# Hybrid encoder layer on one core: four column tiles in the opening, later lane arithmetic, an earlier split of the down activations

## The chip, the core and the metric

One NeuronCore of a Trainium2 chip runs the whole layer as one program. TensorE multiplies; VectorE (DVE in the profile) and ScalarE (ACT) do the elementwise work; GpSimd (POOL) and SyncE (SP) mostly issue DMAs. The metric is the device time of one execution in microseconds; the kernel before takes 2270.38 us (median of 3 runs, 2269.89 to 2271.57).

## The reference, cut to what matters

Two requests of 256 tokens are computed together as T = 512 tokens of width 2048, in float32. The layer is

```
xn    = rmsnorm(x);  proj = xn @ w_in                  # 7200 columns: NA q,k,v; GDN q,k,v; z; b,a
y_na  = neighbourhood_attention(q, k, v)               # 8 heads of 128
y_dn  = gated_deltanet_bidir(conv+silu(q,k,v), z, b, a)  # 8 heads, chunks of 64, both directions
h     = x + [y_na ; y_dn] @ w_out
hn    = rmsnorm(h)
y     = rmsnorm(h + (silu(hn @ w_gate) * (hn @ w_up)) @ w_down)   # 5632 hidden columns
```

In the delta rule each head needs, for each chunk, products of k with k and of k with q, a triangular solve of 64 x 64, and decays made from b and a (the "gates").

## The kernel before, in words

**Products.** Every float32 operand is split in two float32r parts: `hi` is a rounded copy that ScalarE makes, `lo` is the rest that VectorE makes by a subtraction (`split`, L126 to L133). A product is three matmuls, hi by hi, hi by the other's lo, lo by the other's hi (`mm3`, L150), each 128 x 128 weights by 128 x 512 tokens. A column tile (128 output columns) takes 16 k-tiles, thus 48 matmuls (`col_tile`, `half_gemm`); its weights come in two halves of 512 KB over SP's queue into three `raw` buffers and are split into three `hi` and three `lo` buffers.

**The opening** (L223 to L328). 12 small matmuls on ones run while the first data comes. SP's queue loads `nwm`, then a first piece of the weights of column tile 0, x for the first two k-tiles (`xr[0]`, one transfer of 512 KB), the same piece of column tile 1, the weights `ba_raw` of b and a, and then the other seven x transfers with the rest of the two column tiles' weights between them. Column tiles 0 and 1 (k and q of GDN head 0) are multiplied two k-tiles (one pair) at a time for four pairs, then the last eight k-tiles tile by tile. Small matmuls for b and a (`ba_gemm`) follow every fourth k-tile. At the end `token_rstd` squares x (ScalarE), adds the squares up (VectorE), sums over partitions by one matmul on ones and makes `rstd`. x stays in SBUF as hi and lo.

**After the opening.** For GDN heads 0 to 7 the k and q columns are multiplied, convolved and put through silu (`conv_silu`: VectorE scales a tile out of PSUM, and four multiply-adds and two ScalarE operations follow); head 0 takes the two tiles of the opening, the others call `col_tile`. Then come the 24 column tiles of neighbourhood attention, then v and z of the GDN heads with the recurrence. Small work is laid between the matmuls by hand: generators in `chains` and `side` go one step forward with each `pump()`, which `half_gemm` calls after every second k-tile, so eight times a column tile. `kq_post(h)` waits a number of steps (`KQ_START` = 20 for head 0, `KQ_GAP` = 8 for the others), then computes the products of k with k and q through three PSUM tiles of pool `psm` (three banks, tag `s`). Column tiles lie in pool `pg` (three banks).

`gates()` (L385) is traced after head 0's columns: some 45 small VectorE and ScalarE operations with DMAs between them. `lanes()` is the triangular solve: 128 lanes, one per direction, head and chunk, on VectorE. It is started when the last `kq_post` is done, and goes one step forward twice in a column tile (`advance(vector_work)`). Its first step issues ten DMAs that gather `kkq` and `qq`; the arithmetic follows in the next steps (L485 on). Its result goes out to DRAM (L576) and comes back in `prepare` for the recurrence.

**The MLP down product.** The 5632 hidden columns are cut in four segments of 512, done directly (`down`, 8 pairs of output tiles with 24 matmuls per tile pair), and two groups of 14, done by a seven-product Strassen form (`down_group`, j = 0 to 7). The order is `down(0)`, group 0, `down(1)`, group 1, `down(2)`, and the last segment. `down` reads a split activation tile `sA`. While group g runs, `load_act` (L1131) loads the next segment's activations into `sA` by DMA, and at the last j splits them: two ScalarE copies (L1137) and two VectorE subtractions (L1138). In `down_group` this call, `after()`, stands behind the fifth product (`pb`, S2) and the additions that follow it (L1280 to L1283).

**What sets the order.** TensorE's order is that of the program text. On the other engines a planner orders the instructions by its own times: an instruction runs as soon as the planner takes it as ready and its engine as free, and of several the one that was traced first. `tc.high_priority(offset=AHEAD)` lets an instruction count as traced 120 instructions earlier (weight splits use it). `pin` (`keep_in_program_order`) puts an instruction behind the one traced just before it on its engine; the four instructions of `load_act` are pinned. Once planned, each engine's order is fixed.

Of the kernel before, what the change touches and what calls it, by code (L numbers as in the profile page):

```python
# [8 lines left out]
F32 = mybir.dt.float32  # L9
F32R = mybir.dt.float32r  # L10
# [32 lines left out]
NA_START = 5  # L43
NA_GAP = 8
PV_GAP = 4
KQ_START = 20
KQ_GAP = 8
CORE_START = 2
N_GAP = 1
# [13 lines left out]
def hybrid_encoder(ctx: ExitStack, tc: tile.TileContext, xT, w_in, w_ba, w_out, w_gate,  # L63
# [156 lines left out]
    def sm_tile():  # L220
        return psm.tile([P, T], F32, tag="s", name="ps_s")

    kkq = cp.tile([P, C, 2, C], F32, tag="c", name="kkq")  # L223
    rstd = wk.tile([P, T], F32, tag="rstd", name="rstd")


# [2 lines left out]
    xr = [ini.tile([P, 2, T], F32, tag=f"xr{j}", name="x_raw") for j in range(8)]  # L229
    ba_raw = wp.tile([P, KT, 32], F32, tag="raw", bufs=3, name="ba_raw")  # L230
    baw = ini.tile([P, KT, 32], F32, tag="baw", name="ba_w")
    w0 = [[ini.tile([P, 8, P], F32, tag=f"w{c}{i}", name="w0_raw") for i in range(2)]
          for c in range(2)]

    def split_x(j):
        for i in range(2):
            k = 2 * j + i
            split(xs[k][0], xs[k][1], xr[j][:, i], nwm[:, k:k + 1])

    def fetch_w0(i, k0, k1):  # L240
        for c in range(2):
            nc.sync.dma_start(w0[c][i][:, k0:k1], w_in[c, i][:, k0:k1])

    nc.sync.dma_start(w0[0][0][:, :2], w_in[0, 0][:, :2])
    nc.sync.dma_start(xr[0], xT[0])
    nc.sync.dma_start(w0[1][0][:, :2], w_in[1, 0][:, :2])
    nc.sync.dma_start(ba_raw, w_ba)
    for j in range(1, 8):
        nc.sync.dma_start(xr[j], xT[j])
        if j == 1:  # L250
            fetch_w0(0, 2, 8)
        if j == 3:
            fetch_w0(1, 0, 8)

    def token_rstd():
        acc = ini.tile([P, T], F32, tag="acc", name="ssq_acc")
        for k in range(KT):
            sq = acc if k == 0 else ini.tile([P, T], F32, tag="sq", bufs=2, name="x_sq")
            act(out=sq, in_=xr[k // 2][:, k % 2], func=AF.Square)
            if k:  # L260
                tt(acc, acc, sq, ALU.add)
        ps = sm_tile()
        mm(ps, ones, acc, start=True, stop=True)
        rstd_bcast(ps, rstd, ini)
        ini_cm.__exit__(None, None, None)

    def evac(ps, tag, bufs=1, pool=None):
        t = (pool or wk).tile([P, T], F32, tag=tag, bufs=bufs, name="ev_" + tag)
# [6 lines left out]
    def ba_gemm(ks):  # L275
        for k in ks:
            g = k % 4 * 32
            mm(ps_ba[g:g + 32], baw[:, k], xr[k // 2][:, k % 2], start=(k < 4), stop=(k >= KT - 4),
               skip_group_check=True)

    ps_w = sm_tile()
    for _ in range(IDLE):
        mm(ps_w[:, :P], ones, ones, start=True, stop=True)
    ps0 = [pg.tile([P, T], F32, tag="g", name="ps_g") for _ in range(2)]

    def w0_pair(parts):
        hi = wp.tile([P, 8, P], F32R, tag="hi", bufs=3, name="w_hi")
        lo = wp.tile([P, 8, P], F32R, tag="lo", bufs=3, name="w_lo")
        for c, i, k0, k1 in parts:
            split(hi[:, k0:k1], lo[:, k0:k1], w0[c][i][:, k0:k1])  # L290
        return hi, lo

    def first_tiles(c, w, ks):
        for k in ks:
            mm3(ps0[c], w[0][:, k % 8], w[1][:, k % 8], xs[k][0], xs[k][1], k == 0, k == KT - 1)

    hl = [[wp.tile([P, 8, P], F32R, tag=t, bufs=3, name="w_" + t) for t in ("hi", "lo")]
          for _ in range(2)]

    def split_w0(c, k0, k1):  # L300
        split(hl[c][0][:, k0:k1], hl[c][1][:, k0:k1], w0[c][0][:, k0:k1])

    split_w0(0, 0, 2)
    split_x(0)
    split_w0(1, 0, 2)
    for j in range(4):
        ks = (2 * j, 2 * j + 1)
        if j:
            split_x(j)
        if j == 1:  # L310
            for c in range(2):
                split_w0(c, 2, 8)
            tt(baw, ba_raw, nwm[:, :, None].broadcast_to([P, KT, 32]), ALU.mult)
        for c in range(2):
            first_tiles(c, hl[c], ks)
        if j % 2:
            ba_gemm(range(2 * j - 2, 2 * j + 2))
    for j in range(4, 8):
        split_x(j)
    for c in range(2):  # L320
        w = w0_pair([(c, 1, 0, 8)])
        first_tiles(c, w, range(8, KT))
        ba_gemm(range(8 + 4 * c, 12 + 4 * c))
    ps_k0, ps_q0 = ps0
    token_rstd()
    ba = wk.tile([P, T], F32, tag="xi", bufs=2, name="ba")
    tt(ba, ps_ba, rstd, ALU.mult)
    nc.gpsimd.dma_start(s_ba.rearrange("g r t -> (g r) t"), ba)  # L328
# [139 lines left out]
    def lanes():  # L468
# [5 lines left out]
                                .rearrange("d h b k f s c -> (d h b k f) (s c)"))  # L474
        for d in range(2):
            nc.gpsimd.dma_start(qq[half[d]], s_qq.rearrange("h (j t) -> (h j) t", t=C))
        yield


        def vtt(*a):  # L480
# [98 lines left out]

    for h in range(H):  # L580
        kq = wk.tile([P, 2, T], F32, tag="kq", bufs=2, name="kq")
        ps = ps_k0 if h == 0 else col_tile(w_in[2 * h], xs)
        conv_silu(ps, 8 + h, kq[:, 0])
        ps = ps_q0 if h == 0 else col_tile(w_in[2 * h + 1], xs)
# [12 lines left out]
        chains.append(kq_post(h, kq, sqh, sql))  # L597
# [388 lines left out]
    def ahead(lead=AHEAD):  # L986
        return tc.high_priority(offset=lead)
# [252 lines left out]
    def down_group(g, X, sums, after):  # L1240
        A11, A12, A22, S4, S3, S1, S2 = range(7)
        plain = fetch_plain(g, 0)
        for j in range(8):
            first, second = sums
            b11, b21, b22 = plain
            if j < 7:
                sums = fetch_sums(g, j + 1)
                plain = fetch_plain(g, j + 1)
            if g == 1 and j:
                add_residual(j - 1)  # L1250
            h = hT[j].rearrange("p f (b t) -> p (f b) t", b=2)
# [12 lines left out]
            nc.scalar.copy(p7, pc)  # L1264
            with ahead():
                w = w_split(first)
            product(pd, w, X, S1, True)
            tt(d, pd, p7, ALU.subtract)
            with ahead():
                w = w_split(b21)  # L1270
            product(pa, w, X, A12, False, True)
            for q in range(2):
                tt(h[:, 0], h[:, 0], pa[:, q], ALU.add)
            with ahead():
                tt(first, first, b22, ALU.add)
                w = w_split(first)
            product(pb, w, X, S2, True, True)
            u2 = dq.tile([P, L], F32, tag="u2", name="u2d")
            plus_both(u2, p1, pb)
            tt(h[:, 1], h[:, 1], u2, ALU.add)  # L1280
            tt(h[:, 2:], h[:, 2:], u2[:, None, :].broadcast_to([P, 2, L]), ALU.subtract)
            for q in range(2):
                tt(h[:, 3], h[:, 3], d[:, q], ALU.add)  # L1283
            if j == 7:
                after()
            with ahead():
                w = w_split(b22)
# [174 lines left out]
```

## Time and profile before

| | |
|---|---|
| median of 3 runs | 2270.38 us |
| profiled execution: its time, its span | 2270.45 us, 2268.6 us |
| mean granted TensorE clock | 0.997 |
| VectorE, ScalarE, GpSimd busy | 77%, 47%, 16% of the span |
| DMA | 400.77 MB, 177 GB/s over the span |

The span goes from the first to the last instruction. Busy shares are means over stages with different limits. Matmuls overlap in the pipeline, so that one row's duration (about 0.39 us for 512 columns) is longer than the distance from one start to the next. Times are microseconds from the span's start, mean durations in groups are in ns. In a timeline row the first number is the start, the second the duration (of all xN merged), and brackets at the end give the idle time of the engine before it and what ended it. The granted clock is 1.00 at 2.4 GHz and 0.50 at 1.2 GHz.

### The profile page before, as it was taken

Reading aid. Unit: us, or ns where it says so; the run is one execution under the profiler, and the core shown is the slowest. Engines: PE = TensorE matmul, PEld = TensorE weight load, DVE = VectorE, ACT = ScalarE, POOL = GpSimd, SP = SyncE. Lnnn points to the kernel's source line nnn. Section 1 sums busy time; section 2 is a strip of 40 time slices with the busy share of each in tenths; the row PEclk is TensorE's granted clock in tenths of the full one; section 3 lists DMA queues with packets and bytes.
Section 4 is the critical chain, followed back from the end, with each engine's and each line's share of the span. In section 5 each row is a group of like instructions: output and inputs, shape, how many; then the busy total and the mean of one; then the engine's idle time right before and its main releaser. Section 6 shows DMA issues by size and latency. Waiting matters only on the chain.

```text
span 2268.6 us, 32159 instructions
## 1 busy us (share of the span) xinstructions
PE 2247.9 (99%) x12004; PEld 1932.9 (85%) x12004; DVE 1752.7 (77%) x2665; ACT 1056.5 (47%) x1554; POOL 368.1 (16%) x584
## 2 busy tenths in 40 slices
PE   9999999999999999999999999999999999999997
PEld 7888888888888888888888888888888888888877
DVE  7654699994555537888888888888888788898866
ACT  6777232324434416644444444444444454444435
POOL 1423300014433001111111111111010011102100
PEclk9999999999999999999999999999999999999999
DMA  5544522246544547777777777767777577669742
GB/s 207 154 149 138 196 99 91 100 140 180 148 136 135 209 149 237 204 195 214 202 203 200 197 211 186 214 188 213 203 198 185 170 216 184 180 203 219 191 149 75
DMA packets 130124, 400.77 MB, mean 177 GB/s; under 512 B 17664, under 2 KB 30368, under 8 KB 129968
## 3 DMA queue, kind: packets, MB, share of 16 engines
q1 hardware_dynamic: 88576, 271.89, 35.2%
q0 software_dynamic: 41392, 126.83, 25.5%
q8 instruction: 95, 1.56, 0.3%
q14 instruction: 61, 0.50, 0.1%
HBM read 358.47 MB, written 40.17 MB: 176 GB/s over the span
## 4 chain that ended last, share of the span: by engine, by line
PE 97%; DMA 1%; DVE 1%; ACT 0%; issue 0%; SPq 0%; POOL 0%; DVEq 0%; POOLq 0%; ACTq 0%
PE ps_g L75 38%; PE ps_d L75 14%; PE ps_a L75 14%; PE ps_c L75 14%; PE ps_b L75 7%; PE ps_s L75 7%; PE ps_s L78 1%; PE ps_o L75 1%; DMA s_uq<-kkq 0%; DMA nml<-s_na 0%; DMA lead<-s_uq 0%; DVE hT L1357 0%; DMA x_raw<-in_xT_dram 0%; DVE w_lo L130 0%; ACT w_hi L129 0%
## 5 line engine op out<-in xcount | busy, mean ns | idle before, releaser
L75 PE MATMUL ps_g<-xhi,w_hi 128*128 128x512 f32 x896 | 365.1, 408 | 1.0 <-ACT xhi L132 0.5
L75 PE MATMUL ps_g<-xhi,w_lo 128*128 128x512 f32 x896 | 350.0, 391 | 0.4 <-DVE w_lo L130 0.4
L75 PE MATMUL ps_g<-xlo,w_hi 128*128 128x512 f32 x896 | 349.3, 390 | 0.4 <-DVE xlo L133 0.3
L130 DVE TENSOR_TENSOR w_lo<-w_raw,w_hi 128x1024 fp32r<-128x1024 f32 (+2 forms) x170 | 205.5, 1209 | 109.2 <-ACT w_hi L129 97.9
L129 ACT ACTIVATE w_hi<-b 128x1024 fp32r<-128x1024 f32 (+1 forms) x180 | 185.6, 1031 | 221.2 <-issue 99.6
L129 ACT ACTIVATE w_hi<-w_raw 128x1024 fp32r<-128x1024 f32 (+2 forms) x170 | 178.0, 1047 | 219.9 <-PE ps_g L75 174.2
L129 ACT ACTIVATE w_hi<-w_first 128x1024 fp32r<-128x1024 f32 x132 | 140.0, 1061 | 212.0 <-PE ps_c L75 139.5
L130 DVE TENSOR_TENSOR w_lo<-b,w_hi 128x1024 fp32r<-128x1024 f32 (+1 forms) x180 | 212.9, 1183 | 1.5 <-ACT w_hi L129 1.2
L75 PEld LDWEIGHTS ps_g<-xhi,w_lo 128*128 128x128 f32 x896 | 168.2, 188 | 37.7 <-DVE w_lo L130 1.4
L75 PEld LDWEIGHTS ps_g<-xhi,w_hi 128*128 128x128 f32 x896 | 168.5, 188 | 36.6 <-ACT xhi L132 2.5
L75 PEld LDWEIGHTS ps_g<-xlo,w_hi 128*128 128x128 f32 x896 | 168.6, 188 | 32.8 <-DVE xlo L133 1.0
L130 DVE TENSOR_TENSOR w_lo<-w_first,w_hi 128x1024 fp32r<-128x1024 f32 x132 | 161.3, 1222 | 37.2 <-ACT w_hi L129 34.4
L75 PE MATMUL ps_c<-xc,w_hi 128*128 128x512 f32 x704 | 176.7, 393 | 0.0
L75 PE MATMUL ps_d<-xc,w_hi 128*128 128x512 f32 x704 | 176.3, 392 | 0.0
L75 PE MATMUL ps_a<-xc,w_hi 128*128 128x512 f32 x704 | 176.3, 392 | 0.0
L75 PEld LDWEIGHTS ps_c<-xc,w_hi 128*128 128x128 f32 x704 | 126.7, 189 | 23.1 <-issue 0.2
L75 PEld LDWEIGHTS ps_a<-xc,w_hi 128*128 128x128 f32 x704 | 126.7, 189 | 22.7
L75 PEld LDWEIGHTS ps_d<-xc,w_hi 128*128 128x128 f32 x704 | 126.6, 189 | 22.6
L75 PEld LDWEIGHTS ps_c<-xc,w_lo 128*128 128x128 f32 x704 | 96.0, 190 | 6.9
L75 PEld LDWEIGHTS ps_d<-xc,w_lo 128*128 128x128 f32 x704 | 96.0, 190 | 6.9
L75 PEld LDWEIGHTS ps_a<-xc,w_lo 128*128 128x128 f32 x704 | 96.0, 190 | 6.9
L129 ACT ACTIVATE w_hi<-w_two 128x896 fp32r<-128x896 f32 x64 | 61.0, 952 | 86.2 <-PE ps_c L75 31.0
(410 smaller groups left out, 4464.9 us busy)
## 6 DMA issues: line engine op xcount, KB each, us to landing
w_raw<-in_w_in_dram SPq DMA_DIRECT2D x110, 512.0 KB, 3.4
b<-in_w_gate_dram SPq DMA_DIRECT2D x66, 512.0 KB, 3.9
b<-in_w_up_dram SPq DMA_DIRECT2D x66, 512.0 KB, 5.1
b<-in_w_group_dram SPq DMA_DIRECT2D x48, 448.0 KB, 4.9
w_raw<-in_w_out_dram SPq DMA_DIRECT2D x32, 512.0 KB, 3.6
w_raw<-in_w_down_dram SPq DMA_DIRECT2D x32, 512.0 KB, 3.9
w_two<-in_w_group_dram SPq DMA_DIRECT2D x32, 448.0 KB, 5.8
w_two<-in_w_group_dram POOLq DMA_DIRECT2D x32, 448.0 KB, 6.4
```

Of the source, the lines that this page charges most:

```text
L75: pin(nc.tensor.matmul(*a, **k))
L78: pin(nc.tensor.transpose(*a))
L129: act(out=hi, in_=src, func=AF.Copy)
L130: tt(lo, src, r32(hi), ALU.subtract)
```

## The change: what it does

1. The opening multiplies four column tiles (k and q of GDN heads 0 and 1) instead of two, one pair of k-tiles at a time for all eight pairs. Their raw weights lie in one tile `w0` of the pool `cp` (its slot belongs to `kkq` later). On SP's queue each pair's weights (4 x 128 KB, 1 KB per row) go ahead of the pair's x (512 KB); for the first pair the order is weights of tile 0, half of x, weights of tiles 1 to 3, the other half of x. Two of the four accumulators lie in `pg`, two in `psm`.
2. The squares of x are traced two pairs behind the splits, and `token_rstd` before the last pair's matmuls.
3. `KQ_START` goes from 20 to 12; heads 0 and 1 both take tiles of the opening.
4. In `lanes()` three steps instead of one lie between the issue of the gathers and the arithmetic.
5. In `down_group`, `after()` moves from behind the fifth product's additions to behind the fourth product's (L1273).

```diff
-KQ_START = 20
+KQ_START = 12
@@
-    kkq = cp.tile([P, C, 2, C], F32, tag="c", name="kkq")
+    FIRST = 4
+    w0 = cp.tile([P, 8, FIRST, 2, P], F32, tag="c", name="w0_raw")
@@
-    nc.sync.dma_start(w0[0][0][:, :2], w_in[0, 0][:, :2])
-    nc.sync.dma_start(xr[0], xT[0])
-    nc.sync.dma_start(w0[1][0][:, :2], w_in[1, 0][:, :2])
-    nc.sync.dma_start(ba_raw, w_ba)
+    fetch_w0(0, 0, 1)
+    nc.sync.dma_start(xr[0][:, 0], xT[0][:, 0])
+    fetch_w0(0, 1)
+    nc.sync.dma_start(xr[0][:, 1], xT[0][:, 1])
     for j in range(1, 8):
+        fetch_w0(j)
         nc.sync.dma_start(xr[j], xT[j])
         if j == 1:
-            fetch_w0(0, 2, 8)
-        if j == 3:
-            fetch_w0(1, 0, 8)
+            nc.sync.dma_start(ba_raw, w_ba)
@@
-    ps0 = [pg.tile([P, T], F32, tag="g", name="ps_g") for _ in range(2)]
...
+    ps0 = [pg.tile([P, T], F32, tag="g", name="ps_g") for _ in range(2)] + [sm_tile(), sm_tile()]
+
+    for j in range(8):
+        hi = wp.tile([P, FIRST, 2, P], F32R, tag="hi", bufs=3, name="w_hi")
+        lo = wp.tile([P, FIRST, 2, P], F32R, tag="lo", bufs=3, name="w_lo")
...
+        def first_tiles(i):
+            k = 2 * j + i
+            for c in range(FIRST):
+                mm3(ps0[c], hi[:, c, i], lo[:, c, i], xs[k][0], xs[k][1], k == 0, k == KT - 1)
+
+        if j == 0:
+            split_w0(0, 1)
+            split_x(j, (0,))
+            split_w0(1, FIRST)
+            split_x(j, (1,))
+        else:
+            split_w0(0, FIRST)
             split_x(j)
         if j == 1:
             tt(baw, ba_raw, nwm[:, :, None].broadcast_to([P, KT, 32]), ALU.mult)
+        if j > 1:
+            square_x(j - 2)
+        if j == 7:
+            square_x(6)
+            square_x(7)
+            token_rstd()
+        for i in range(2):
+            first_tiles(i)
         if j % 2:
             ba_gemm(range(2 * j - 2, 2 * j + 2))
...
+    kkq = cp.tile([P, C, 2, C], F32, tag="c", name="kkq")
+    ini_cm.__exit__(None, None, None)
@@ lanes
-        yield
+        yield from pause(3)
@@ heads of k and q
-        ps = ps_k0 if h == 0 else col_tile(w_in[2 * h], xs)
+        ps = ps0[2 * h] if h < 2 else col_tile(w_in[2 * h], xs)
@@ down_group
             for q in range(2):
                 tt(h[:, 0], h[:, 0], pa[:, q], ALU.add)
+            if j == 7:
+                after()
             with ahead():
                 tt(first, first, b22, ALU.add)
...
             for q in range(2):
                 tt(h[:, 3], h[:, 3], d[:, q], ALU.add)
-            if j == 7:
-                after()
```

## Rows read from the trace of the kernel before

**Rows 1.** The page's busy times: us, share of the span, instructions.
```profile
PE 2247.9 (99%) x12004; PEld 1932.9 (85%) x12004; DVE 1752.7 (77%) x2665; ACT 1056.5 (47%) x1554; POOL 368.1 (16%) x584
```

**Rows 2.** Waits of TensorE: what waited, for what; total us, times, longest.
```profile
PE ps_g L75 <- DVE aA L1138: 4.8, 2, 3.6
...
PE ps_o L75 <- ACT n L788: 0.6, 1, 0.6
...
PE ps_s L78 <- ACT dvT L344: 0.3, 1, 0.3
```

**Rows 3.** Chain of waits in order of time: start, us, what.
```profile
1.65 4.52 DMA x_raw<-in_xT_dram
...
37.34 29.96 PE ps_g L75 x132
...
538.88 0.84 PE ps_s L75 x8
```

**Rows 4.** Instruction groups, 0 to 37.3 us: count, busy us, mean ns, idle before.
```profile
L133 DVE SCALAR_TENSOR_TENSOR xlo<-x_raw,nwm,xhi 128x512 fp32r<-128x512 f32 x16 | 11.0, 745 | 2.5 <-ACT xhi L132 2.5
L132 ACT ACTIVATE xhi<-x_raw,nwm 128x512 fp32r<-128x512 f32 x16 | 10.4, 710 | 2.2 <-DMA x_raw<-in_xT_dram 2.2
L261 DVE TENSOR_TENSOR ssq_acc<-ssq_acc,x_sq 128x512 f32<-128x512 f32 x15 | 10.3, 688 | 0.6
L259 ACT ACTIVATE x_sq<-x_raw 128x512 f32<-128x512 f32 x15 | 9.3, 622 | 1.9 <-DVE ssq_acc L261 1.9
...
L130 DVE TENSOR_TENSOR w_lo<-w_raw,w_hi 128x1024 fp32r<-128x1024 f32 x5 | 6.1, 1220 | 1.0 <-ACT w_hi L129 1.0
...
L129 ACT ACTIVATE w_hi<-w_raw 128x1024 fp32r<-128x1024 f32 x5 | 5.3, 1054 | 2.1 <-PE ps_g L75 2.1
...
L75 PE MATMUL ps_ba<-x_raw,ba_w 128*32 128x512 f32 x32 | 4.3, 605 | 0.0
...
L130 DVE TENSOR_TENSOR w_lo<-w_raw,w_hi 128x768 fp32r<-128x768 f32 x2 | 1.9, 954 | 0.0
...
L75 PE MATMUL ps_s<-ssq_acc,ones 128*128 128x512 f32 x2 | 1.1, 645 | 0.0
```

**Rows 5.** Timeline of the opening, TensorE's small matmuls and its first product.
```profile
1.05 5.49 PE L75 MATMUL ps_s<-ones 128*128 128x128 f32 x24 [1.05 <-DVE epsc L98]
...
7.04 0.50 PE L75 MATMUL ps_g<-xhi,w_hi 128*128 128x512 f32 x1 [0.49 <-ACT xhi L132]
```

**Rows 6.** Windows: length, busy per engine (count), granted clock, DMA share, GB/s.
```profile
12.00:17.00 5.00, 4.78 (x23) 2.89 (x24) 5.00 (x9) 5.00 (x9) 0.14 (x2) 1.00 1.03 410
503.00:506.00 3.00, 3.00 (x17) 2.49 (x16) 2.38 (x3) 1.53 (x2) 3.00 (x3) 1.00 1.02 283
2162.00:2168.00 6.00, 6.00 (x15) 4.77 (x16) 3.71 (x6) 3.06 (x3) 1.22 (x1) 0.54 0.88 274
```

**Rows 7.** Timeline where `down(1)` (1977) and `down(2)` (2158) begin, TensorE and VectorE.
```profile
1977.58 0.50 PE L75 MATMUL ps_g<-aA,w_hi 128*128 128x512 f32 x1 [1.19 <-DVE aA L1138]
...
2152.19 0.41 DVE L1273 TENSOR_TENSOR hT<-hT,ps_a 128x256 f32<-128x256 f32 x1
...
2160.73 2.35 DVE L1138 TENSOR_TENSOR aA<-aA 128x1024 fp32r<-128x1024 f32 x2
...
2162.00 0.80 PE L75 MATMUL ps_g<-aA,w_hi 128*128 128x512 f32 x1 [3.62 <-DVE aA L1138]
```

**Rows 8.** Timeline in `down(2)`, weight splits before its fourth pair.
```profile
2171.68 1.06 ACT L129 ACTIVATE wd<-w_raw 128x1024 fp32r<-128x1024 f32 x1 [4.30 <-DMA w_raw<-in_w_down_dram]
...
2173.91 1.22 DVE L130 TENSOR_TENSOR w_lo<-w_raw,w_hi 128x1024 fp32r<-128x1024 f32 x1
```

**Rows 9.** Timeline of VectorE: two operations of `lanes()` and one of `prepare(0)`.
```profile
83.19 0.20 DVE L500 COPY egkq<-ega 128x64 f32<-128x64 f32 x1
...
250.78 0.22 DVE L485 TENSOR_SCALAR nkx<-kkq 128x64 f32<-128x64 f32 x1 [8.12 <-DMA qq<-s_qq]
...
536.29 0.43 DVE L750 TENSOR_TENSOR u_tail<-u_tail,scs 128x256 f32<-128x256 f32 x1 [4.72 <-DMA u_tail<-s_uq]
```

More of the change, by code (lines that the diff above doesn't have):

```diff
@@ L231, in hybrid_encoder, with split_x, fetch_w0, square_x @@
     baw = ini.tile([P, KT, 32], F32, tag="baw", name="ba_w")
[L232 to L236, printed above, removed]
+    def split_x(j, ks=(0, 1)):
+        for i in ks:
             k = 2 * j + i
             split(xs[k][0], xs[k][1], xr[j][:, i], nwm[:, k:k + 1])
-    def fetch_w0(i, k0, k1):
-        for c in range(2):
-            nc.sync.dma_start(w0[c][i][:, k0:k1], w_in[c, i][:, k0:k1])
-    nc.sync.dma_start(w0[0][0][:, :2], w_in[0, 0][:, :2])
-    nc.sync.dma_start(xr[0], xT[0])
-    nc.sync.dma_start(w0[1][0][:, :2], w_in[1, 0][:, :2])
-    nc.sync.dma_start(ba_raw, w_ba)
+    def fetch_w0(j, c0=0, c1=FIRST):
+        k = j % 4 * 2
+        nc.sync.dma_start(w0[:, j, c0:c1].rearrange("p c k n -> p c (k n)"),
+                          w_in[c0:c1, j // 4].rearrange("c p k n -> p c (k n)")
+                          [:, :, k * P:(k + 2) * P])
+    fetch_w0(0, 0, 1)
+    nc.sync.dma_start(xr[0][:, 0], xT[0][:, 0])
+    fetch_w0(0, 1)
+    nc.sync.dma_start(xr[0][:, 1], xT[0][:, 1])
     for j in range(1, 8):
+        fetch_w0(j)
         nc.sync.dma_start(xr[j], xT[j])
         if j == 1:
-            fetch_w0(0, 2, 8)
-        if j == 3:
-            fetch_w0(1, 0, 8)
-    def token_rstd():
-        acc = ini.tile([P, T], F32, tag="acc", name="ssq_acc")
-        for k in range(KT):
+            nc.sync.dma_start(ba_raw, w_ba)
+    acc = ini.tile([P, T], F32, tag="acc", name="ssq_acc")
+    def square_x(j):
+        for k in (2 * j, 2 * j + 1):
             sq = acc if k == 0 else ini.tile([P, T], F32, tag="sq", bufs=2, name="x_sq")
-            act(out=sq, in_=xr[k // 2][:, k % 2], func=AF.Square)
+            act(out=sq, in_=xr[j][:, k % 2], func=AF.Square)
             if k:
                 tt(acc, acc, sq, ALU.add)
+    def token_rstd():
         ps = sm_tile()
@@ L264, in token_rstd @@
         rstd_bcast(ps, rstd, ini)
-        ini_cm.__exit__(None, None, None)
     def evac(ps, tag, bufs=1, pool=None):
@@ L283, in hybrid_encoder @@
         mm(ps_w[:, :P], ones, ones, start=True, stop=True)
-    ps0 = [pg.tile([P, T], F32, tag="g", name="ps_g") for _ in range(2)]
[L286 to L308, printed above, removed]
+    ps0 = [pg.tile([P, T], F32, tag="g", name="ps_g") for _ in range(2)] + [sm_tile(), sm_tile()]
+    for j in range(8):
+        hi = wp.tile([P, FIRST, 2, P], F32R, tag="hi", bufs=3, name="w_hi")
+        lo = wp.tile([P, FIRST, 2, P], F32R, tag="lo", bufs=3, name="w_lo")
+        def split_w0(c0, c1):
+            split(hi[:, c0:c1], lo[:, c0:c1], w0[:, j, c0:c1])
+        def first_tiles(i):
[9 more added lines that the diff above has]
+            split_w0(0, FIRST)
@@ L309, in hybrid_encoder @@
             split_x(j)
         if j == 1:
-            for c in range(2):
-                split_w0(c, 2, 8)
             tt(baw, ba_raw, nwm[:, :, None].broadcast_to([P, KT, 32]), ALU.mult)
-        for c in range(2):
-            first_tiles(c, hl[c], ks)
+        if j > 1:
[6 more added lines that the diff above has]
+            first_tiles(i)
         if j % 2:
             ba_gemm(range(2 * j - 2, 2 * j + 2))
-    for j in range(4, 8):
-        split_x(j)
@@ L320, in hybrid_encoder @@
[L320 to L325, printed above, removed]
+    kkq = cp.tile([P, C, 2, C], F32, tag="c", name="kkq")
+    ini_cm.__exit__(None, None, None)
     ba = wk.tile([P, T], F32, tag="xi", bufs=2, name="ba")
@@ L581, in hybrid_encoder @@
         kq = wk.tile([P, 2, T], F32, tag="kq", bufs=2, name="kq")
-        ps = ps_k0 if h == 0 else col_tile(w_in[2 * h], xs)
+        ps = ps0[2 * h] if h < 2 else col_tile(w_in[2 * h], xs)
         conv_silu(ps, 8 + h, kq[:, 0])
-        ps = ps_q0 if h == 0 else col_tile(w_in[2 * h + 1], xs)
+        ps = ps0[2 * h + 1] if h < 2 else col_tile(w_in[2 * h + 1], xs)
         conv_silu(ps, h, kq[:, 1])
```

## The prediction

> **What bounds the kernel.** I read the page's busy times first: TensorE has work in 99% of the span [rows 1], so nothing can be won except where TensorE stands still or runs slowly. The windows along the span show it full from 40 to 1900 us, with losses at the start and at two places near the end. The waits of TensorE name the largest: 4.8 us in two waits, the longest 3.6, for VectorE's subtraction on `aA` (L1138) [rows 2]. They lie where `down(1)` and `down(2)` begin [rows 7]. For the opening the busy share hides the stalls, since the shown duration of a matmul is longer than the distance of two starts. There I count: in the chain 132 matmuls of 512 columns take 29.96 us, 0.227 us each [rows 3]. From the first product at 7.04 [rows 5] to 37.34 [rows 3], 30.3 us, lie 97 such matmuls (22.0 us), the b and a matmuls (4.3) and the sum over partitions (1.1) [rows 4], together 27.4. So 2.9 us of the opening are stall.
>
> **The opening.** No matmul is added or removed: two column tiles move from behind the opening into it. What changes is the start and the stalls.
>
> The start: x of the first pair lands at 1.65 + 4.52 = 6.17 us [rows 3]. Half of it is 256 KB less, at 410 GB/s [rows 6] 0.64 us: 5.5. ScalarE's copy (0.65, 10.4 / 16 [rows 4]) ends at 6.2. But the matmuls on ones stand ahead on TensorE and end at 1.05 + 5.49 = 6.54, where the wait of 0.49 before the first product begins [rows 5]. So the start comes 0.5 us earlier and no more.
>
> The first pair: xlo of k-tile 0 is ready at about 6.9 (VectorE 0.7 after the copy), the second matmul waits 0.2. The weights of tiles 1 to 3 (384 KB) land 1.0 us after the half of x at 410 GB/s, or 1.4 at the 283 GB/s that the nearest transfers in small pieces (512 B, the write-out of `kkq`) reach in the second window of [rows 6]: 6.5 to 6.9. ScalarE 0.8 (three quarters of 1.05), VectorE 0.95 [rows 4]: hi at 7.3 to 7.8, lo at 8.3 to 8.7; TensorE, past tile 0 at 7.4, waits 0.4 to 1.2 in all. The other half of x lands 0.64 later, is split by 9.4, and is wanted at about 10. Stalls here: 0.6 to 1.2, I take 0.9.
>
> From the second pair on TensorE needs 24 x 0.227 + half of a b-and-a batch (1.07 / 2) = 6.0 us per pair. DMA brings 1 MB in 2.6 us at 410 GB/s, 3.2 if the weights move at 283. ScalarE has 1.05 + 2 x 0.65 + 2 x 0.62 = 3.6, VectorE 1.22 + 2 x 0.69 + 2 x 0.69 = 4.0 [rows 4]. All are hidden; only the second pair is close (split by 12 to 12.8, wanted at 13). The squares end some 40 us into the run, before TensorE comes to the sum ahead of pair 8 at about 49. Gain: 0.5 + (2.9 - 0.9) = 2.5 us. At most it is 0.5 + 2.9 = 3.4; at least, with stalls of 1.2 and a second pair that is late by 0.7, 1.5.
>
> The page "DMA: Bandwidth & Descriptors" of the Trainium skill (Rules for kernel authors; Anatomy of one DMA) advises transfers of 1 MiB or more and puts about 2 us of fixed cost on each; four transfers where three served the first pair would by that alone leave a gain of 0.5. The trace has 512 KB transfers behind each other at 410 GB/s with the DMA engines full [rows 6], so in a full queue the fixed part overlaps. The case in which it doesn't is rival 2.
>
> **The heads after it.** Heads 0 and 1 are convolved together while TensorE runs head 2. The first Gram products come after 12 to 15 of `pump`'s steps, of 6 x 0.227 = 1.36 us, thus 16 to 20 us after the opening. By then two banks of `psm` must be free of column tiles. VectorE has four convolutions to do from there, each some 4 us of its time, and the gates; I take it as in time, cost 0 (rival 4 is the case that it isn't). The chains of the later heads then end 12 steps into the attention tiles, before and after the change alike, so the gathers go out where they did, relative to TensorE.
>
> **The lanes.** VectorE stands 8.12 us before the first lane operation, at 250.78, for the gathered `qq` [rows 9]. Two more steps are one column tile, 48 x 0.227 = 10.9 us and small matmuls, about 12. But the planner lets an operation run when it takes it as ready, not where it is traced: L500 of `lanes()` ran at 83.19, 168 us before the others [rows 9]. So the wait may well stay. If it goes, nobody gains at once: TensorE isn't waiting there. If the start really moves by 12 us, it lands 3.9 us later than now (12 - 8.1); VectorE has hardly a gap from there to the end of the lanes, so the recurrence would have its inputs 3.9 later. There `u_tail` is ready at 536.29 + 0.43 = 536.7 [rows 9] and TensorE wants it at 538.88 [rows 3]: 2.2 us of slack, a cost of up to 1.7. I take 0; at the good end two small waits of TensorE in the recurrence go, 0.3 and 0.6 [rows 2].
>
> **The down activations.** The activations lie in SBUF over 100 us ahead, and ScalarE's copies are made 11 us ahead. Only the two subtractions are late: the first is pinned behind the last addition before `after()`, L1283, and lands behind two weight splits at 2160.73 [rows 7]. Moved, the pin is L1273, which at `down(2)` runs at 2152.19. From 2152.6 the 2.35 us of the pair are done by 2155, or 2157.5 if two weight splits (1.22 each) of higher priority go first. The first matmul that needs them starts at 2158.0 (the wait of 3.62 ends at 2162.00, 2158.38 when it began [rows 7], the first product 0.4 before). What is queued behind them on VectorE, additions into `hT`, `u2` and the splits for `down`, goes back by at most 2.35 - 0.7 of idle time; the first split there ends by 2156.5, still in time.
>
> Saved at `down(1)`: 1.19 idle [rows 7]. Saved at `down(2)`: 3.62 idle, and the clock. In 2162 to 2168, right behind the wait, the granted clock is 0.54 [rows 6], which is nearly all at 1.2 GHz; 15 matmuls run in those 6 us where 6 / 0.227 = 26 would, 11 x 0.227 = 2.6 us lost. Together 6.2.
>
> What is late next in `down(2)`: its fourth pair of tiles. TensorE would come there at 2158.0 + 3 x 24 x 0.227 = 2174.3 and wants the lo weights at 2174.8. They were made from 2173.91 to 2175.1, behind a copy on ScalarE that waited 4.30 us for a DMA [rows 8], whose buffer VectorE freed; that chain doesn't follow TensorE, and the earlier subtractions may push it by up to 1.2. So a new wait of 0.4 to 1.6, I take 0.9. `down(2)` saves 5.3 (4.6 to 6.2).
>
> **Sum.** 2.5 + 1.2 + 5.3 = 9.0 us. The profiled execution took 2270.45 (span 2268.6), the median is 2270.38: the same within 0.1. Forecast 2270.4 - 9.0 = 2261.4 us; its own range, with 3.4, 1.2, 6.2 and 0.9 saved at one end and 1.5, 1.2, 4.6 saved and 1.7 lost at the other: 2258.7 to 2264.8.
>
> **Rivals.**
> 1. *The wait in `down(2)` moves instead of going*: its weight chain (fourth and later pairs) is as late as before and TensorE catches up with it; for it speaks that ScalarE's waits there end with a DMA [rows 8], against it that the later pairs' splits lie ahead of the new need. Saving at `down(2)` about 2.5: 2264.2.
> 2. *The opening's split transfers are served one by one.* The x transfer took 4.52 us where its bytes need 1.3 [rows 3, 6]; 3.2 us again before the first pair is complete leaves 2.5 - 3.2 = -0.7: 2264.6. Against it: the full queue.
> 3. *The change doesn't do what it says at the down product*: the planner still puts the subtractions behind weight splits. Then only the opening counts: 2267.9. Against it: nothing older than the splits stands ahead of them.
> 4. *Slower: PSUM in the opening.* Two of three `psm` banks hold columns of head 1. Where VectorE and ScalarE, strictly in their planned order, do head 0's gates first, those banks come free late. The gates ran until 83.2 [rows 9], 46 us after the opening's end at 37.3; if head 1's evacuation stood behind them, TensorE would wait from 20 to some 40 us after the opening: 20 us and a slow clock after it (2.6): 2270.4 - 9.0 + 22.6 = 2284. It decides from a wait of about 9 us on; below, it only eats gain. Against it: head 1's columns are ready at once, and the planner prefers what is ready.
>
> **How the numbers follow.** Forecast 0.62, rival 1 0.13, rival 2 0.10, rival 3 0.08, rival 4 0.07. Two runs of this kernel can be told apart from about 0.2%, 4.5 us, so faster means below 2265.8: the forecast, rivals 1 and 2 nearly whole, 0.83; same: rival 3 and edges, 0.10; slower 0.07. The range runs from 2257.5 to 2266.5: the forecast's ends and rivals 1 and 2, with 1 to 2 us around them for the new order that the planner makes of everything; it leaves out rivals 3 and 4.
>
> **What would show it.** Opening: first product at about 6.5, four column tiles and the sum done by about 57 us with stalls near 1 us. Heads: no wait of TensorE for a `ps_s` bank between 60 and 95. Lanes: the 8 us wait of VectorE there or not, and `u_tail` against its matmul. Down: L1138 behind L1273 and ahead of the additions, no wait of TensorE for `aA`, granted clock 1.00 through both seams, a short wait for `w_lo` some 16 us into `down(2)`. Wrong it would be if TensorE waits in 60 to 95 us, if the clock falls at any new place, or if L1138 is still last.

## The result and the profile after

The changed kernel takes 2291.26 us (median of 4 runs, 2289.59 to 2292.4) where the kernel before takes 2270.39 beside it: ratio 1.0091 [1.0073, 1.0108], 21 us slower. The forecast was 2261.4 (2257.5 to 2266.5), with 0.07 for slower. The profiled execution took 2292.4 us, its span is 2290.6. Lines of the changed kernel are five lower than before from `conv_silu` on (L1138 is L1133, L485 is L480).

The page's busy times answer to [rows 1]: TensorE's share falls by one point, no other engine has more to do.

```profile
PE 2252.1 (98%) x12004; PEld 1935.5 (84%) x12004; DVE 1752.3 (76%) x2664; ACT 1057.4 (46%) x1553; POOL 368.5 (16%) x584
```

The waits of TensorE after the change (columns as in [rows 2]). The wait for `aA` is gone, as forecast. Four of these five were not there before, and the one for `w_lo` was 0.4.

```profile
PE ps_s L78 <- DMA lead<-s_uq: 9.9, 1, 9.9
PE ps_g L75 <- DVE w_lo L130: 4.8, 3, 4.1
PE ps_a L75 <- DVE xd L130: 4.3, 1, 4.3
PE ps_s L75 <- ACT kq L339: 2.2, 1, 2.2
PE ps_s L75 <- DVE hT L1291: 1.6, 1, 1.6
```

Where they lie, from TensorE's timeline after the change; among them are the places that answer to [rows 5] and [rows 7]: the opening's first product (5.90), and the first matmuls of `down(1)` (1997) and of `down(2)` (2186), which start without a wait.

```profile
1.06 5.07 PE L75 MATMUL ps_s<-ones 128*128 128x128 f32 x24 [1.06 <-DVE epsc L98]
5.90 0.50 PE L75 MATMUL ps_g<-xhi,w_hi 128*128 128x512 f32 x1
6.69 0.50 PE L75 MATMUL ps_g<-xlo,w_hi 128*128 128x512 f32 x1 [0.28 <-DVE xlo L133]
...
147.18 1.13 PE L75 MATMUL ps_s<-kq 128*128 128x256 f32 x4 [2.22 <-ACT kq L339]
...
264.28 0.50 PE L75 MATMUL ps_g<-xhi,w_lo 128*128 128x512 f32 x1 [4.05 <-DVE w_lo L130]
...
546.10 1.09 PE L78 MATMUL ps_s<-ident,lead 128*128 128x128 f32 x4 [9.93 <-DMA lead<-s_uq]
...
1997.05 0.63 PE L75 MATMUL ps_g<-aA,w_hi 128*128 128x512 f32 x2
...
2186.37 0.63 PE L75 MATMUL ps_g<-aA,w_hi 128*128 128x512 f32 x2
```

Windows after the change (columns as in [rows 6]): behind three of the waits the granted clock falls to its lower level (the first window begins ahead of the fall), and where `down(2)` begins, 0.54 before [rows 6], it is now 1.00.

```profile
261.00:267.00 6.00, 2.72 (x8) 2.14 (x9) 5.90 (x34) 0.00 (x0) 1.80 (x4) 0.83 0.28 88
546.00:552.00 6.00, 5.90 (x17) 4.82 (x18) 1.65 (x2) 1.64 (x2) 5.75 (x10) 0.53 0.46 107
2048.00:2054.00 6.00, 5.73 (x20) 4.99 (x21) 5.47 (x8) 2.99 (x4) 0.87 (x1) 0.54 0.50 176
2186.00:2192.00 6.00, 6.00 (x30) 5.04 (x29) 5.75 (x11) 1.75 (x2) 1.12 (x2) 1.00 0.74 236
```

TensorE's order is the same text in both kernels, but for the opening, the Gram products of the first four heads (up to 135 us) and the lanes' four transposes. So the start of the same matmul in both traces gives a running account, after minus before. A wait is counted here with the slow restart of the next matmuls, so that it is 0.1 to 0.3 us more than in the rows above:

| place (time before) | delay there, us | what it adds |
|---|---|---|
| head 2's first column tile (58.98) | -2.3 | the opening: 2.3 won |
| Gram product of head 4 (146.95) | +0.2 | 2.4 wait for `kq`, 0.1 of order |
| head 6's columns (186.85) | +1.3 | 0.8 wait for `w_lo`, 0.3 in small steps |
| attention tiles (263.99) | +7.0 | 4.2 wait for `w_lo`, 1.5 slow clock |
| `dvT` (525.93) | +7.8 | 0.75 more wait for `dvT` |
| `lead` (528.25) | +17.9 | 10.1 wait for `lead` |
| behind it (531 on) | +20.5 | 2.6 slow clock |
| `down(1)` begins (1977.58) | +19.7 | 0.4 lost on the way, 1.2 won |
| inside `down(1)` (1991.09) | +21.3 | 1.6 wait for a PSUM bank (`hT`) |
| group 1 begins (2022.37) | +25.9 | 4.6 wait for `xd` |
| behind it | +28.4 | 2.5 slow clock |
| inside `down(2)` (2166.86) | +22.3 | 6.1 won |
| end | +21.9 | 0.4 won, the last of the slow clock before |

Three stories, thus: the opening wins 2.3 and then loses 9.3 up to 270; the lanes cost some 13; the down product wins 7.7 and loses 8.7. The experiments take them one by one. Runs of the kernel before beside them had medians of 2270.3 to 2271.3.

### The profile page after: what moved, and what is told of

Same layout as the page of the kernel before. It is cut to its first block, busy times and chain, and to the rows that moved or that the text cites. A ratio compares the mean times of both kernels' runs of the same rounds, so it can differ in the third digit from the quotient of the medians.

```text
span 2290.6 us, 32164 instructions
## 1 busy us (share of the span) xinstructions
PE 2252.1 (98%) x12004; PEld 1935.5 (84%) x12004; DVE 1752.3 (76%) x2664; ACT 1057.4 (46%) x1553; POOL 368.5 (16%) x584
## 4 chain that ended last, share of the span: by engine, by line
PE 87%; ACT 4%; DVE 3%; DMA 3%; issue 2%; POOL 1%; SPq 0%; ACTq 0%; DVEq 0%; POOLq 0%
PE ps_g L75 30%; PE ps_a L75 14%; PE ps_d L75 14%; PE ps_c L75 14%; PE ps_b L75 7%; PE ps_s L75 6%; DVE cacc L337 1%; PE ps_s L78 1%; DVE w_lo L130 1%; PE ps_o L75 1%; ACT E L458 1%; ACT w_hi L129 1%; ACT E L460 1%; DMA kkq<-s_gram 1%; DVE kkq L476 1%
## 5 line engine op out<-in xcount | busy, mean ns | idle before, releaser
L75 PE MATMUL ps_g<-xhi,w_hi 128*128 128x512 f32 x864 | 354.6, 410 | 0.0
L75 PE MATMUL ps_g<-xhi,w_lo 128*128 128x512 f32 x864 | 339.0, 392 | 4.8 <-DVE w_lo L130 4.8
L75 PE MATMUL ps_g<-xlo,w_hi 128*128 128x512 f32 x864 | 338.3, 392 | 0.3 <-DVE xlo L133 0.3
L130 DVE TENSOR_TENSOR w_lo<-w_raw,w_hi 128x1024 fp32r<-128x1024 f32 (+1 forms) x169 | 205.1, 1214 | 121.5 <-ACT w_hi L129 105.8
L129 ACT ACTIVATE w_hi<-w_raw 128x1024 fp32r<-128x1024 f32 (+1 forms) x169 | 177.6, 1051 | 229.0 <-PE ps_g L75 180.0
L75 PEld LDWEIGHTS ps_g<-xhi,w_lo 128*128 128x128 f32 x864 | 163.1, 189 | 41.7 <-DVE w_lo L130 6.1
L75 PEld LDWEIGHTS ps_g<-xhi,w_hi 128*128 128x128 f32 x864 | 163.5, 189 | 35.3 <-ACT w_hi L129 3.2
L75 PEld LDWEIGHTS ps_g<-xlo,w_hi 128*128 128x128 f32 x864 | 163.6, 189 | 31.6 <-DVE xlo L133 0.8
L130 DVE TENSOR_TENSOR w_lo<-w_first,w_hi 128x1024 fp32r<-128x1024 f32 x132 | 161.3, 1222 | 37.3 <-ACT w_hi L129 32.1
```

The lines of the kernel that those rows point to most:

```text
L75: pin(nc.tensor.matmul(*a, **k))
```

## The experiments

**1. Each part alone.** Four kernels, one chip.

```diff
# e1: before, with only this
+            if j == 7:
+                after()          # behind the fourth product (and no longer behind the fifth)
# e2: after, with          # e3: e2, and after() behind the fifth product again
-        yield from pause(3)
+        yield
# e4: before, with only
-        yield
+        yield from pause(3)
```

Expected of the down move alone: 

> The kernel before with the fifth part of the change alone: the down activations are split behind the fourth product. Theory (the move makes its own new wait): it gains 1.2 us where down(1) begins and 6.2 where down(2) begins, as forecast, and loses in down(1) what the changed kernel lost there, 1.6 for a PSUM bank and 4.3 plus 2.4 of slow clock for xd, because the order of ScalarE in down(1) has a copy of xd that waits for a DMA ahead of a weight split: 2270.4 - 7.5 + 8.6, thus 2270 to 2273, with a wait of TensorE for xd of about 4 us. Rival (those waits of the changed kernel come from its earlier parts, which shift everything by 20 us): no wait for xd, 2270.4 - 7.5, thus 2262 to 2264.

Expected without the two added lane steps: 

> The changed kernel with one step instead of three between the gathers and the lane arithmetic. Theory (the two added steps alone put the solve back): the four transposes of the lanes stand one column tile earlier in TensorE's order, the solve on VectorE begins some 15 us earlier than at 310, lead comes in time, and the wait of 10 us for it goes with the 2.6 us of slow clock behind it: 2291 - 12.7 = 2278.6 (2276 to 2281); the stall of 4 us for w_lo near 260 stays. Rival (the gather itself, late since the opening changed, makes the lanes late, and the steps do nothing, as the prediction had it): lead is still late by 5 us or more, 2284 to 2290.

Expected of the opening alone: 

> The opening alone (parts 1 to 3 of the change): no added steps in the lanes, the down activations split where they were. Theory: the opening gains 2.3 us, and then loses 3.6 among the heads and 5.7 near 260 (4.2 of wait for w_lo behind the late gathers, 1.5 of slow clock): 2270.4 + 7.0 = 2277.4 (2275 to 2280), with ScalarE's Gram copies some 10 us behind their products in heads 3 to 6, where they were 5.7 before. Rival (the stalls among the heads and near 260 come with the added steps): the gain of 2.3 us stands, 2267 to 2270.

Expected of the lane steps alone: 

> The kernel before with the fourth part alone: three steps between the gathers and the lane arithmetic. Theory (the two steps are one column tile for everything that is pinned in TensorE's and VectorE's order behind them): the wait of 8 us for the gathers stays, the solve begins 12 to 17 us later than at 285, lead is late for TensorE by 6 to 12 us: 2279 to 2285 with the clock. Rival, the prediction's: the planner takes the operations as they come ready, the lanes end as before, 2269 to 2272.

| | median, us | ratio to before |
|---|---|---|
| e1 down move alone | 2270.45 | 1.0001 [0.9991, 1.001] |
| e2 after, without the steps | 2279.46 | 1.0038 [1.0024, 1.0052] |
| e3 opening alone | 2280.52 | 1.0043 [1.0028, 1.0058] |
| e4 lane steps alone | 2282.08 | 1.005 [1.0035, 1.0065] |

All four went by the first theory (e3 half a microsecond above its range). The parts nearly add: 9.3 (e3) + 10.8 (e4) - 0.8 (e1) = 19.3 of the 20.9.

*The lane steps.* In e4 TensorE waits for `lead` as it does after the change, with nothing else changed.

```profile
PE ps_s L78 <- DMA lead<-s_uq: 7.8, 1, 7.8
```

Without the steps (e2) that wait is absent. VectorE's timeline shows how. These two rows are of the changed kernel, the second of them the start of the solve.

```profile
258.21 0.22 DVE L480 TENSOR_SCALAR nkx<-kkq 128x64 f32<-128x64 f32 x1 [14.21 <-DMA kkq<-s_gram]
...
310.21 0.11 DVE L547 MEMSET W<- 64x64 f32 x1
```

The first lane operation runs the moment the gathers land, steps or no steps: it is not pinned. But the multiplications of `kkq` by E and by `ndm` are pinned. The last of them and the start of the solve, in the kernel before:

```profile
281.48 1.23 DVE L481 TENSOR_TENSOR kkq<-kkq,ndm 128x1024 f32<-128x1024 f32 x1
...
285.28 0.11 DVE L552 MEMSET W<- 64x64 f32 x1
```

In e4 the last ones stand behind the scores of an attention head, for which VectorE waits:

```profile
289.49 0.49 DVE L623 TENSOR_TENSOR na_s<-ps_s,bias 128x320 f32<-128x320 f32 x1 [4.36 <-PE ps_s L75]
...
298.95 1.23 DVE L481 TENSOR_TENSOR kkq<-kkq,ndm 128x1024 f32<-128x1024 f32 x1
...
303.03 0.11 DVE L552 MEMSET W<- 64x64 f32 x1
```

The solve begins 2.6 to 2.9 us behind the end of the last multiplication in each of these kernels: at 303.0 in e4 (17.7 later than before, with the gathers where they were), at 294.4 in e3, at 310.2 with both changes. The lanes' four transposes, which the steps moved 48 matmuls back in TensorE's text, do not hold it: in the kernel before (the row below, of TensorE) and in e3 they run 4.2 us after the solve has begun.

```profile
289.44 0.27 PE L78 MATMUL ps_s<-ident,k 128*128 128x128 f32 x1
```

*The opening.* e3 shows the wait of 5.7 us for `w_lo` near 260 and the one of 2.3 for `kq` without the steps. Two rows of ScalarE, one trace each: the copy of head 7's Gram products out of PSUM, before and after. The products stand at 219.05 and 220.40, so that the copy follows them by 3.8 us before and by 8.0 after.

```profile
222.89 1.06 ACT L363 COPY gs<-ps_s 128x512 f32<-128x512 f32 x2
```

```profile
228.44 1.05 ACT L358 COPY gs<-ps_s 128x512 f32<-128x512 f32 x2
```

The gathers follow the copies, so they land 7.4 us later, and VectorE, which waits for them at the head of its queue, has a weight split behind the wait and the lane operations: `w_lo` comes at 263.01 and TensorE at 264.28 [4.05 <-DVE w_lo].

*The down move.* In e1 as after the change, `down(1)` pays for the seams. Three rows of e1, two of ScalarE and one of VectorE: ScalarE stands 8 us in front of a copy of `a_spare`, whose transfer has not landed, with a weight split queued behind it; VectorE stands 6.7 us for that split, with the additions behind it that free PSUM and the sums for group 1.

```profile
1987.69 0.85 ACT L129 ACTIVATE xd<-a_spare 128x768 fp32r<-128x768 f32 x1 [8.03 <-DMA a_spare<-s_act]
1988.45 1.04 ACT L129 ACTIVATE w_hi<-w_raw 128x1024 fp32r<-128x1024 f32 x1
...
1989.52 1.22 DVE L130 TENSOR_TENSOR w_lo<-w_raw,w_hi 128x1024 fp32r<-128x1024 f32 x1 [6.73 <-ACT w_hi L129]
```

TensorE then waits, in e1:

```profile
PE ps_a L75 <- DVE xd L130: 3.2, 1, 3.2
PE ps_s L75 <- DVE hT L1296: 1.5, 1, 1.5
```

**2. One seam only, and what makes ScalarE late.**

```diff
# e5: before, with the early after() for g == 1 only
# e6: e3, with
-        for s in range(s0, s1):          # decays
+        for s in range(s0, s1, 2):
# e7: e3, with KQ_START = 20
# e8: e3, with FIRST = 2 (two column tiles in pg, head 1 by col_tile), KQ_START = 20
```

> The kernel before, with the down activations split behind the fourth product in the second group only (ahead of down(2)); at down(1) the call stays behind the fifth. Theory (the loss of the early split lies in down(1) alone, in the order that ScalarE gets there, and nothing of it in down(2)): the 6.2 us of down(2) stay gained, no wait for xd: 2271 - 6.2 = 2264.8, 2263 to 2266.5. Rival (group 1 loses as much elsewhere once its seam goes early): 2268 to 2272.

> The opening alone, as in the run of parts 1 to 3, with every second pair of the decay exponentials of heads 2 to 7 left out (their entries of E stay zero): some 3.6 us less for ScalarE per head. Theory (four convolutions behind the opening put ScalarE and VectorE behind TensorE, and a head's chain of convolution, exponentials and weight copies is as long as TensorE's 24 us, so that they never catch up): with room in it they do; the Gram copies of heads 4 to 7 follow their products by 6 us or less, the gathers land by 250, and the waits at 147, 182 and 260 go with the slow clock: 2271 - 2 = 2269, 2268 to 2271. Rival (the gathers are late and the weight split stands behind them for another reason, the new buffers or DMA traffic): the wait of 5.7 us near 260 stays, 2276 to 2281.

> The opening alone with KQ_START back at 20, so that the Gram products of the first heads come eight steps (11 us) later. Theory (ScalarE sets the pace up to the gathers): the wait of 2.3 us for kq at 147 goes, but ScalarE's chain ends where it did and the wait near 260 grows by as much: 2280 again, 2278 to 2282. Rival (the Gram products were put too early and the waits start there): 2274 to 2278.

> The new opening with two column tiles instead of four (weights ahead of x, squares two pairs behind the splits, w0 of half the size; head 1 by col_tile, KQ_START 20). Theory (the transfers and the order are good, the four tiles are what costs, since head 0's convolutions start 20 us later with them): eight pairs of 12 x 0.227 + 0.53 = 3.3 us end near 33 instead of 37, no wait near 147 or 260: 2271 - 3, 2267 to 2270. Rival (weights in small pieces and squares among the splits hold TensorE up): 2271 to 2275.

| | median, us | ratio to before |
|---|---|---|
| e5 second seam only | 2264.9 | 0.9975 [0.9965, 0.9985] |
| e6 half the decays left out | 2267.87 | 0.9985 [0.9976, 0.9994] |
| e7 KQ_START 20 | 2281.24 | 1.0044 [1.003, 1.0058] |
| e8 two tiles | 2278.31 | 1.0031 [1.0019, 1.0043] |

e5 keeps what `down(2)` gains and loses nothing; the 1.2 us at `down(1)` stay. In e6 the Gram copies again wait for their products (the first row below, of ScalarE), the first lane operation runs at 246.69 instead of 258.61, and TensorE's largest wait for a weight split is 0.3 us; it stays 2.0 to 2.3 us ahead of the kernel before from 140 us up to the seams. (Another 0.9 us of the gain in e6's profile does not come from the decays: behind the wait at `down(2)` the clock was slow for a shorter time in that execution.) In e7 the wait for `kq` went and two others came, 7.4 us in all for weight splits where e3 has 6.9: moving the Gram products shifts only the place at which TensorE meets ScalarE. So what keeps the gathers late is the work that ScalarE has per head, not the buffers, the transfers or the place of the products.

```profile
218.09 0.59 ACT L358 COPY gs<-ps_s 128x512 f32<-128x512 f32 x1 [0.79 <-PE ps_s L75]
```

```profile
PE ps_g L75 <- DVE w_lo L130: 3.8, 3, 3.1
PE ps_g L75 <- ACT w_hi L129: 3.6, 2, 3.0
```

e8 missed: slower by 7 us, by neither theory. It has no wait near 147 or 260, as the theory wanted, but lost in the opening itself: the sum over partitions stands ahead of the last pair in TensorE's text, and the squares are not summed by then (head 1's columns start at 43.24, before at 36.77).

```profile
36.50 2.07 PE L75 MATMUL ps_s<-ssq_acc,ones 128*128 128x512 f32 x2 [5.17 <-DVE ssq_acc L261]
```

**3. Three repairs.**

```diff
# e9: e3 with DECAY_ROWS = 8, early after() for g == 1 only, and in the attention's head 0
+            decays(48, 56)      # behind its q tile
+            decays(56, 64)      # behind its k tile
# e10: e8 with token_rstd() behind the last pair's matmuls, early after() for g == 1 only
# e11: before with the early after() at both seams, and in make(n)
-            split(x[:, :3, 0], x[:, :3, 1], raw[:, 1:])
+            hi = act(out=x[:, :3, 0], in_=raw[:, 1:], func=AF.Copy)
+            if g:
+                pin(hi)
+            tt(x[:, :3, 1], raw[:, 1:], r32(x[:, :3, 0]), ALU.subtract)
```

> The four-tile opening with the decay exponentials thinned out and nothing left out: heads 2 to 7 make 8 rows of E each instead of 11, and the last 16 rows are traced behind the first two column tiles of the attention; the down activations are split early in the second group only. Theory (ScalarE's 24 us per head leave no room to catch up after the opening; 3 rows less are 2 us of room per head): the waits at 147, 182 and 260 shrink to 2 us or less together, so that the opening keeps its 2 us: 2271 - 2 - 6.2 = 2263, 2261.5 to 2265. Rival (2 us a head are too little, or ScalarE is then late in the attention tiles): the gathers are still late, a wait for w_lo of 3 us or more near 260 with its slow clock, 2267 to 2273.

> The opening with two column tiles, the sum of squares traced behind the last pair's matmuls instead of ahead of them, and the down activations split early in the second group only. Theory (the 5.2 us for ssq_acc with two tiles came from the place of that sum in TensorE's order, while the squares needed until 36): the last pair fills the wait, head 1 starts 1 to 2 us earlier than before: 2271 - 6.2 - 1.5 = 2263.3, 2262 to 2265. Rival (the opening is bound by ScalarE's and VectorE's squares and splits and the wait only moves behind the pair): no gain over the early split alone, 2265 to 2268.

> The kernel before with the early split at both seams, and in down(1) the first copy of every xd kept behind the weight split that is traced ahead of it. In ScalarE's order that swaps the copy of a_spare and the fourth weight split. Theory (ScalarE waited 8 us for the DMA of a_spare with a weight split that was ready queued behind it, and VectorE behind that): no idle of VectorE for w_hi of 6 us, no wait of TensorE for hT, and the one for xd at the start of group 1 shrinks to 1 us or less: 2271 - 7.5, 2263 to 2266. Rival (the a_spare transfer itself is late, whatever stands behind it): xd is still late by 3 us, 2268 to 2271.

| | median, us | ratio to before |
|---|---|---|
| e9 decays spread | 2272.63 | 1.0008 [1.0, 1.0017] |
| e10 two tiles, sum last | 2268.61 | 0.9992 [0.9982, 1.0001] |
| e11 pinned copy | 2265.05 | 0.9972 [0.9961, 0.9983] |

e9 went by its rival. The Gram copies of heads 4 to 6 came 0.4 to 2.2 us earlier than before the change, so ScalarE had caught up; but the planner drew the rows that were meant for the attention tiles in front of head 7's copies and between them (ScalarE of e9):

```profile
226.37 0.57 ACT L358 COPY gs<-ps_s 128x512 f32<-128x512 f32 x1
226.96 0.34 ACT L460 ACTIVATE E<-G,NG 64x57 f32<-64x57 f32 x1
...
228.85 0.56 ACT L358 COPY gs<-ps_s 128x512 f32<-128x512 f32 x1
```

and TensorE waited 6.9 us for `w_lo` again. e10 went by its rival too, 0.6 above its range: with the sum last, TensorE still waits 2.58 us for it, and head 1's columns start at 38.65. I read it so that with two tiles the splits and squares of ScalarE and VectorE bound the opening, since a pair of k-tiles then has only half the matmuls to hide them behind; no run here leaves them out.

e11 went by its theory. In ScalarE's order the weight split now runs first, and the copy waits behind it for its transfer, where that holds nobody up; TensorE's waits for `hT`, `xd` and `aA` are all gone, and TensorE is 6.7 us ahead of the kernel before at the end. By the medians it is no faster than e5, which leaves the seam at `down(1)` as it was; so the 1.2 us there show in the trace and not in the time.

```profile
1981.71 1.06 ACT L129 ACTIVATE w_hi<-w_raw 128x1024 fp32r<-128x1024 f32 x1 [1.28 <-PE ps_s L75]
1986.90 0.85 ACT L1201 ACTIVATE xd<-a_spare 128x768 fp32r<-128x768 f32 x1 [4.13 <-DMA a_spare<-s_act]
```

**4. All of it together.**

```diff
# e12: e3 with DECAY_ROWS = 9, e11's changes, and in kq_post behind qrow's copy
         if h == H - 1:
+            decays(6 * DECAY_ROWS, C)
```

> What the runs so far point to, in one kernel: the four-tile opening, 9 rows of E per head instead of 11 and the other 10 rows on ScalarE behind head 7's last copy out of PSUM (so that they stand in front of no Gram copy), no added steps in the lanes, the early split at both seams with the first copy of xd kept behind the weight split in down(1). Theory (the opening's gain of 2 us holds if ScalarE has room among the heads and the gathers are not delayed; the seams give 6.7): the Gram copies of head 7 come where they came before, the wait near 260 is 1 us or less: 2271 - 2 - 6.7 = 2262, 2260.5 to 2264. Rival (the gathers are still some microseconds late, or the 10 rows in a block hold the weight copies of the first attention tiles): a wait for w_lo or w_hi of 3 us or more between 220 and 270 with its slow clock, 2266 to 2271.

2264.93 us, ratio 0.9976 [0.9967, 0.9985]: faster than before, but 1 us above the theory's range and no better than e5 or e11 with the old opening. The waits near 147, 182 and 260 are gone (the largest for a weight split is 0.7 us, and head 7's copies follow at 225.15). Two things ate the gain: a wait for `xd` of 1.6 us at group 1, which e11 did not have, and, in the execution that was profiled, an opening that was 2.3 us later than e3's and so 0.5 later than before. That execution took 2267.21, more than the median, so how much the opening gives in the others is not shown; but the fastest of the eleven (2264.07) is no faster than e11's fastest (2263.66).

```profile
PE ps_a L75 <- DVE xd L1200: 1.6, 1, 1.6
```

## Why the prediction was wrong

**The opening: the gain right, its parts not.** Four tiles were done 2.3 us earlier than before (forecast 2.5). But the start gave 1.1 of it (forecast 0.5), and the stalls went from 2.9 to 1.8 by the prediction's own count (192 x 0.227 + 4.3 + 1.1 = 49.0 of the 50.8 us from 5.90 to 56.69), which gives 1.2 (forecast 2.0): that the sum came out is in part luck. The first pair's waits were about 1 us, as forecast; so some 0.8 of what was counted as stall lies elsewhere and stayed. The first product began at 5.90, not 6.5, while the last row of matmuls on ones was still shown as running until 6.13. A row's end is no end for the next start, as the prediction itself had said of the long matmuls. The gain is also not the same in each execution: with the same opening, head 2 began 1.7 to 2.3 us earlier than before in the profiles of the changed kernel, e2, e3, e6, e7 and e9, and 0.5 later in that of e12.

**The step that failed first: "VectorE has four convolutions to do from there, each some 4 us of its time, and the gates; I take it as in time, cost 0".** It was priced as VectorE's time alone and against one deadline, the first Gram products, which were indeed in time. But a convolution goes back and forth between ScalarE and VectorE (copy, four multiply-adds, silu), and head 0's began some 16 us later than before. From head 2 on ScalarE has a head's two convolutions, 11 rows of E (22 exponentials) and the weight copies to do in the 24 us that TensorE takes. Its own rows are not the whole of it: in the 24 us from 179 on, after the change, they fill 18.5, but 5.2 more it stands for VectorE's multiply-adds, whose results come next in its order.

```profile
179.00:203.00 24.00, 23.47 (x103) 18.67 (x102) 12.47 (x15) 18.52 (x37) 8.15 (x14) 1.00 0.44 143
```

```profile
ACT kq L339 <- DVE cacc L337: 3.8, 1, 3.8
ACT L339 <- DVE cacc L337: 1.4, 1, 1.4
```

Together that is 23.7 of 24.0: no room. The Gram copies of heads 2 to 7 came 16.6, 12.0, 6.8, 5.5, 5.5 and 5.5 us later than before, so from head 5 on nothing more was made up. e6 shows that room is what lacked: with half the exponentials out of the way the copies of heads 4 to 7 came 4.4 to 6.3 us earlier than before, and TensorE kept the opening's 2 us. (The planner makes a new order with each such edit; e9, with 8 rows of E for 11, bears e6 out up to head 6.) The lateness cost 3.6 us among the heads and 5.7 near 260. The price of 0 should have been a sum over ScalarE's rows of one head, with its waits for VectorE between them, against 24 us.

**"So the gathers go out where they did, relative to TensorE": failed with it.** The products did (the same place in TensorE's text), the copies behind them came 4.2 us later relative to TensorE. The gathers wait for the copies.

**The lanes: "it lands 3.9 us later than now", "a cost of up to 1.7. I take 0".** The solve began 17.7 us later in e4, and `lead` cost 8.0 us and 2.6 of slow clock. The argument rested on one row, L500 at 83.19 [rows 9], an operation that is not pinned and needs no gather. What decides are the pinned multiplications. For them two steps are one column tile, some 12 us, whatever is ready, and the 8.1 us of VectorE's wait is not taken off, since it lies ahead of them; 4.4 more are the wait for the attention scores behind which the last of them now stand. The slack of 2.2 us at `u_tail` was read rightly, but TensorE's input was later than that by far.

**The down product: `down(2)` right, `down(1)` half seen.** L1133 runs behind L1268 (2180.90 behind 2180.57), no wait for `aA`, the clock at 1.00; 6.5 us won (forecast 5.3), and the wait of 0.9 in the fourth pair did not come. What the clock gives back there depends on the execution: behind the same wait of 3.62 us the next 6 us were at 0.54 in the kernel before, but at 0.72 to 0.75 in e3, e4, e6, e7 and e8. At `down(1)` the 1.2 us came, but the prediction looked at what stands behind the moved subtractions on VectorE only. The planner made a new order for ScalarE too, some ten instructions further on, and 8.7 us were lost there (e1: the whole move gives nothing; e11: one pin gives most of it back).

**The rivals.** Rival 4 had the sign, and about the time, but not the mechanism: no PSUM bank of `psm` was waited for between 60 and 95 us. Its idea, work that runs late in a planned order, came true at another resource and much later in the run; that the gates were what made it late is not shown. Rivals 1 to 3 did not occur. Of the signs under "Wrong it would be", the second, "if the clock falls at any new place", is what happened, at three places.

## What to carry to other kernels

When a change makes work of another engine start later, ask whether that engine has room to catch up before the next thing that depends on it: sum its rows over one period, add the waits for other engines that stand between them, and hold the whole against the period of the bounding engine (here 18.5 and 5.2 against 24.0; the rows alone would have promised room). With no room, the delay travels until something waits for it. When traced steps are inserted, sort what follows into pinned and free; only the free part runs when it is ready. And where a planner fixes in-order queues, look after every move for an instruction that waits for a transfer with a ready weight split behind it: one pin there was worth some 5 us (e1 against e11).

## What the runs showed of the hardware that was not expected

The granted clock fell to its lower level behind TensorE's waits of 4.1, 9.9 and 4.3 us, at a further cost of 1.5, 2.6 and 2.5 us, and behind shorter ones: 3.2 us in e1 (0.62 from 2026 to 2030) and 2.8 in e2 (0.67 from 2035 to 2040). One and the same wait had it both ways. At the Gram product of head 4 TensorE waited 2.22 us in the changed kernel and 2.31 in e3, and the clock stayed at 1.00; in e2 it waited 2.29 (the first row), and the next 6 us were at 0.72 (the second).

```profile
147.82 0.48 PE L75 MATMUL ps_s<-kq 128*128 128x256 f32 x1 [2.29 <-ACT kq L339]
```

```profile
148.00:154.00 6.00, 6.00 (x20) 4.76 (x21) 1.83 (x2) 5.87 (x13) 2.19 (x4) 0.72 0.81 268
```

In the opening of e12 it fell too, to 0.59 between 11 and 14 us (below), though no stall there was longer than 1 us; e3 and the changed kernel, with the same opening, stayed at 1.00. The first weights of tiles 1 to 3 were copied from 7.84 us on in that execution and from 6.50 on in the changed kernel's, so transfers that are first on the queue landed more than 1 us apart from one execution to the next.

```profile
11.00:14.00 3.00, 3.00 (x10) 2.34 (x9) 2.57 (x4) 2.79 (x6) 0.00 (x0) 0.59 1.06 377
```

The page "DMA: Bandwidth & Descriptors" of the Trainium skill (Anatomy of one DMA) fits a fixed cost of about 2 us per transfer, on transfers that GpSimd issues. The prediction's estimate from it, a gain of only 0.5 in the opening, did not come true: with four small transfers on SP's queue where three had been, the first product came 1.1 us earlier and the opening gained 2.3.
